# A Mamba-2 recurrence on one core: another PSUM bank for the state's product, and a split diagonal for the group norm's roots

## The chip, the core and the metric

The kernel runs on one core of a Trainium2 chip. The metric is the device time of one execution in microseconds, here the median of three runs. A profiled execution of the same program gives the trace.

The names of the engines in the profile: PE is TensorE (matmuls), PEld is its weight load, DVE is VectorE, ACT is ScalarE, POOL is GpSimd and SP is SyncE, which here only issues DMA transfers. SBUF is the core's working memory. PSUM is the memory into which TensorE writes, eight banks of 128 partitions by 512 float32.

## The reference

A trunk of two layers over 1040 tokens (16 learned tokens and 1024 given ones) of width 1024, in float32. Each layer has a mixer and a convolutional feed-forward part, each between two RMS norms. Layer 0 mixes with a gated linear recurrence beside sliding-window attention. Layer 1, which the change concerns, is a Mamba-2 mixer:

```
z, x, B, C, dt = split(u @ w_in)              # z, x: 2048 wide; B, C: 8 groups x 128; dt: 32 heads
x, B, C = silu(causal_conv4(x, B, C))
for each of 8 groups, with 4 heads of 64 and a state of 128 x 64 a head:
    h[t] = exp(dt[t] * A) * h[t-1] + dt[t] * outer(B[t], x[t])
    y[t] = C[t] . h[t] + D * x[t]
y = y * silu(z)
y = y * rsqrt(mean over the group's 256 channels of y^2 + 1e-6) * w
out = y @ w_out
```

The recurrence is computed in blocks of tokens: inside a block by products of matrices, from block to block through the state.

## The kernel before

**Products.** A float32 GEMM product is made as three matmuls of a reduced float32 type (fp32r in the profile): weights and activations are split into a high and a low half, and high by high, high by low and low by high are summed (`mm3`, lines L251 to L253). Matmuls with plain float32 operands show as two records each.

**Phases.** Layer 0's mixer and feed-forward part, an early share of layer 1's input GEMM, the recurrence with the rest of that GEMM (some 1690 to 2289 us of the span), the output GEMM (tiles `op`) and layer 1's feed-forward part. The order of instructions on each engine is set when the kernel is built: a scheduler places them by priority and by its own estimate of times, and each engine then works through its queue in that order.

**The recurrence.** The loop goes over eight groups:

```python
for g in range(8):
    ssd(g)
    if g > 0:
        z_and_gate(g - 1)
    if g < 7:
        new_tiles(g + 1, range(4))
        make(g + 1, range(4))
z_and_gate(7)
```

`make(g, js)` computes the group's tiles B, C, x0 and x1 (channels by 1040 tokens; `z0` and `z1` for j of 4 and 5) by GEMM, in three chunks of 348 and 346 tokens. The GEMM's PSUM tiles `ps_g` rotate through two banks. `conv4` evacuates them: ACT copies a chunk into a tile `xs_s` (L580, two buffers), ACT takes the first tap (L587) and DVE the other three (L589). Each of x0 and x1 has two buffers, one for even and one for odd groups, so x0 of group g + 2 is written where x0 of group g stood, once that one has been written out. The first taps of x of group g + 2 therefore wait for group g's write to memory.

`ssd(g)` goes over nine blocks of 16 and 8 x 128 tokens. A block's tiles in PSUM have a bank each: `seg` (decays, L1174 and L1181), `tr` (C times B and the transposes of x and B, L1186 and L1188), `py` (outputs: C times the state, L1202, and the block's own part, L1214), and `pst`, which holds the state's product in its upper half (L1204) and the transposes of y in its lower half (L1223). DVE and ACT work between: `wt`, `xdt`, `xw`, the state `st` (POOL's decay L1210, DVE's sum L1211, L1208 in a first block), `y` (L1218, L1219), and L1225 adds y to x.

`gate(g)` multiplies x by z (L1231, DVE, 1026 columns) and then, in three chunks of 342 tokens, squares on ACT (`gsq`, L1236), adds on POOL (L1238) and calls `token_rsqrt`: TensorE sums over channels (`pst_gn`, L178), DVE adds the epsilon (`rs_gn`, L186), POOL takes the power -1/2 (`rr_gn`, L188), and TensorE spreads the root over the partitions by three products with the identity (`rb_gn`, L192). DVE multiplies x by it (L1241). Then x goes to the tensor `zd` in memory (L1244, DMA), from where the output GEMM reads it as `zr`, split by ACT into `zh` (L630) and by DVE into `zl` (L631). `pst_gn` and `rb_gn` take turns in the two banks of the pool `k.pb`; the GEMM's `ps` have two banks and `seg`, `tr`, `py` and `pst` one each, eight in all.

Of the kernel before, what the change touches and what calls it, by code (L numbers as in the profile page):

```python
# [13 lines left out]
F32 = mybir.dt.float32  # L14
F32R = mybir.dt.float32r
AF = mybir.ActivationFunctionType
ALU = mybir.AluOpType
# [4 lines left out]
P = 128  # L22
# [111 lines left out]
def token_blocks(n):  # L134
    nb = (n + 127) // 128
    w = (n + nb - 1) // nb
    return nb, w, [min(j * w, n - w) for j in range(nb)]
# [36 lines left out]
def token_rsqrt(k, acc, col, n, name):  # L174
    nb, w, st = token_blocks(n)
    pst = k.pb.tile([P, 512], F32, tag="pb", name=f"pst_{name}")
    for j in range(nb):
        k.nc.tensor.matmul(pst[:w, j:j + 1], lhsT=acc[:, st[j]:st[j] + w], rhs=col, start=True, stop=True)  # L178
    return rsqrt_rows(k, pst, n, name)


def rsqrt_rows(k, pst, n, name):
    nc = k.nc
    nb, w, st = token_blocks(n)
    s = k.small.tile([P, 4], F32, tag="rs", bufs=3, name=f"rs_{name}")
    nc.vector.tensor_scalar(s[:w, :nb], pst[:w, :nb], 1e-6, None, ALU.add)  # L186
    r = k.small.tile([P, 4], F32, tag="rr", bufs=3, name=f"rr_{name}")
    nc.gpsimd.tensor_tensor(r[:w, :nb], s[:w, :nb], k.mhalf[:w, :nb], ALU.pow)  # L188
    rb = k.pb.tile([P, 512], F32, tag="pb", name=f"rb_{name}")
    for j in range(nb):  # L190
        o = j * w - st[j]
        nc.tensor.matmul(rb[:, j * w:st[j] + w], lhsT=r[:w, j:j + 1].broadcast_to([w, P]),  # L192
                         rhs=k.ident[:w, o:w], start=True, stop=True)
    return rb


# [831 lines left out]
def mixer1(k, W, V, zd, pd):  # L1028
    nc, tc = k.nc, k.tc
    I = k.I  # L1030
    with ExitStack() as es:
# [42 lines left out]
        def dt_chunk(ci, wdt):  # L1074

            t0, n = TCH[ci]
            ps = pp.tile([P, 512], F32, tag="ps", name=f"dtp{ci}")
            for kk in range(NK):
                w = wdt[:, kk * 64:(kk + 1) * 64]
                for i, u in enumerate((k.uh, k.ul)):  # L1080
                    nc.tensor.matmul(ps[:64, :n], lhsT=w, rhs=u[:, kk, t0:t0 + n], start=kk + i == 0, stop=kk + i == NK)
            nc.scalar.copy(dtr[:, t0:t0 + n], ps[:64, :n])
# [82 lines left out]
        def ssd(g):  # L1165
# [4 lines left out]
            for b, (t0, w) in enumerate(BLK):  # L1170
# [30 lines left out]
                if b > 0:  # L1201
                    nc.tensor.matmul(py[:w, 256:512], lhsT=C[:, tk], rhs=st.rearrange("p a b -> p (a b)"), start=True, stop=True)  # L1202
                if b < 8:
                    nc.tensor.matmul(pst[:, 256:512], lhsT=bt[:w], rhs=xw[:w].rearrange("p a b -> p (a b)"), start=True, stop=True)  # L1204
                    ps4 = pst[:, 256:512].rearrange("p (h d) -> p h d", h=4)
                    st2 = t([P, 4, 64], "st", 2, f"st{g}_{b}")
                    if b == 0:
                        nc.scalar.copy(st2, ps4)  # L1208
                    else:
                        nc.gpsimd.tensor_tensor(st2, st, bc(dec, P, b, 64), ALU.mult)  # L1210
                        nc.vector.tensor_tensor(st2, st2, ps4, ALU.add)  # L1211
                    st = st2
# [15 lines left out]
        def gate(g):  # L1228
# [3 lines left out]
            for ci, (t0, n) in enumerate(C1):  # L1232
# [3 lines left out]
                    nc.scalar.activation(s[:, :n], xx[:, t0:t0 + n], AF.Square)  # L1236
                    sq.append(s)
                nc.gpsimd.tensor_tensor(sq[0][:, :n], sq[0][:, :n], sq[1][:, :n], ALU.add)  # L1238
                rb = token_rsqrt(k, sq[0], k.mean_g, n, f"gn{g}_{ci}")
                for j, xx in enumerate((x0, x1)):  # L1240
                    nc.vector.scalar_tensor_tensor(xx[:, t0:t0 + n], xx[:, t0:t0 + n], V["gn"][:, 2 * g + j:2 * g + j + 1],  # L1241
                                                   rb[:, :n], ALU.mult, ALU.mult)
# [117 lines left out]
def build(tc, I, O):  # L1360
# [17 lines left out]
    with ExitStack() as es:  # L1378
# [7 lines left out]
        k.ident = const.tile([P, P], F32, name="ident")  # L1386
        k.mhalf = const.tile([P, 4], F32, name="mhalf"); nc.vector.memset(k.mhalf, -0.5)
        k.tiny = const.tile([P, 1], F32, name="tiny"); nc.vector.memset(k.tiny, 1e-34)
        k.mean_d = const.tile([P, 1], F32, name="mean_d"); nc.vector.memset(k.mean_d, 1 / 1024)
        k.mean_g = const.tile([P, 1], F32, name="mean_g"); nc.vector.memset(k.mean_g, 1 / 256)  # L1390
        off, nv = vec_layout()
# [66 lines left out]
```

## Time and profile before

| | us |
|---|---|
| runs | 3224.03, 3220.53, 3223.37; median 3223.37 |
| profiled execution | 3219.36 |
| its span (first to last instruction) | 3217.5 |
| TensorE's matmuls busy | 3151.6 |
| TensorE's weight loads busy | 3040.0 |
| DVE busy | 2125.0 |
| ACT busy | 1663.5 |
| POOL busy | 456.9 |

The mean granted clock of TensorE over the span is 0.992. Matmuls are pipelined, so that TensorE's busy time in the profile overlaps itself, and a time from one matmul to the next is read from the starts in the timeline. Line numbers in the rows are those of the kernel before; `ps_g<-uh,whi` reads: tile `ps_g` is written from `uh` and `whi`.

### The profile page before, as it was taken

The page shows a single profiled execution, that of the slowest core. Times are in us where ns is not written, and L with a number is a line of the kernel's source. Part 1 is how long each engine was busy: PE and PEld are TensorE (multiplying, and loading weights), DVE is VectorE, ACT ScalarE, POOL GpSimd, SP SyncE. Part 2 cuts the span into 40 slices and gives each one's busy share as a digit, 9 for nine tenths or more (in the row PEclk, how much of TensorE's full clock was granted, in tenths as well). Part 3 has the DMA queues.
Part 4 walks back from the last instruction along what each step waited for, and adds up shares of the span by engine and source line. Part 5 has one row for each costly group of instructions (what it writes and reads, how often), then busy time and mean ns, then how long its engine had stood idle before and what let it go on. Part 6 is the DMA issues. An engine that isn't in the chain of part 4 may idle for free.

```text
span 3217.5 us, 57030 instructions
## 1 busy us (share of the span) xinstructions
PE 3151.6 (98%) x21886; PEld 3040.0 (94%) x21886; DVE 2125.0 (66%) x3998; ACT 1663.5 (52%) x3119; POOL 456.9 (14%) x772
## 2 busy tenths in 40 slices
PE   8999999999999999999999999999999999999998
PEld 7888877999999999999999998999899999999998
DVE  6663334566988885654677767776655798887553
ACT  6764445554544445543446655556455544445442
POOL 3110000332200000320001122221232300000000
PEclk9999999999999999999999999999899999999999
DMA  4221102674322236765432112111466522225673
GB/s 131 80 68 52 35 30 81 190 238 159 111 86 80 77 112 218 231 205 162 140 118 67 40 64 81 63 53 61 145 209 213 159 80 80 80 80 173 199 221 123
DMA packets 186513, 385.71 MB, mean 120 GB/s; under 512 B 22368, under 2 KB 114688, under 8 KB 186240
## 3 DMA queue, kind: packets, MB, share of 16 engines
q1 hardware_dynamic: 186240, 382.06, 37.2%
q8 instruction: 172, 2.82, 0.4%
q14 instruction: 101, 0.83, 0.1%
HBM read 300.89 MB, written 80.50 MB: 119 GB/s over the span
## 4 chain that ended last, share of the span: by engine, by line
PE 85%; issue 4%; ACT 4%; DMA 3%; DVE 3%; POOL 1%; POOLq 0%; SPq 0%; DVEq 0%; ACTq 0%
PE dn L251 4%; PE dn L252 4%; PE dn L253 4%; PE ps_g L252 4%; PE ps_g L251 4%; PE ps_g L253 4%; PE op L253 2%; PE op L252 2%; PE op L251 2%; DMA zr<-zd 2%; PE upS1up L251 2%; PE upS3up L251 2%; PE upA11up L251 2%; PE upA11up L253 2%; PE upS1up L252 2%
## 5 line engine op out<-in xcount | busy, mean ns | idle before, releaser
L108 DVE TENSOR_TENSOR wlo<-wst,whi 128x1024 fp32r<-128x1024 f32 x304 | 379.5, 1251 | 320.9 <-ACT whi L107 293.2
L107 ACT CAST whi<-wst 128x1024 fp32r<-128x1024 f32 x305 | 318.3, 1045 | 376.7 <-PE dn L252 190.0
L251 PE MATMUL dn<-mid,whi 128*128 128x346 f32 (+3 forms) x1056 | 339.0, 321 | 0.0
L253 PE MATMUL dn<-mid,wlo 128*128 128x346 f32 (+3 forms) x1056 | 338.4, 320 | 0.0
L252 PE MATMUL dn<-mid,whi 128*128 128x346 f32 (+3 forms) x1056 | 338.3, 320 | 0.0
L251 PE MATMUL ps_g<-uh,whi 128*128 128x346 f32 (+1 forms) x864 | 288.9, 334 | 1.1 <-ACT xs_s L580 1.1
L252 PE MATMUL ps_g<-ul,whi 128*128 128x346 f32 (+1 forms) x864 | 285.8, 331 | 0.0
L253 PE MATMUL ps_g<-uh,wlo 128*128 128x346 f32 (+1 forms) x864 | 284.2, 329 | 0.2 <-DVE wlo L108 0.2
L253 PE MATMUL op<-zh,wlo 128*128 128x342 f32 (+2 forms) x768 | 249.0, 325 | 2.3 <-DVE wlo L108 2.3
L252 PE MATMUL op<-zl,whi 128*128 128x342 f32 (+2 forms) x768 | 249.0, 325 | 0.9 <-DVE zl L631 0.9
L251 PE MATMUL op<-zh,whi 128*128 128x342 f32 (+2 forms) x768 | 244.3, 325 | 4.1 <-ACT zh L630 3.3
L82 ACT CAST wb<-wst 128x512 fp32r<-128x512 f32 x270 | 165.8, 619 | 131.3 <-PE upS3up L253 57.3
L83 DVE TENSOR_TENSOR wb<-wst,wb 128x512 fp32r<-128x512 f32 x270 | 185.4, 688 | 42.4 <-ACT wb L82 42.3
L252 PEld LDWEIGHTS dn<-mid,whi 128*128 128x128 f32 x1056 | 199.3, 189 | 0.0
L251 PEld LDWEIGHTS dn<-mid,whi 128*128 128x128 f32 x1056 | 199.2, 189 | 0.0
L253 PEld LDWEIGHTS dn<-mid,wlo 128*128 128x128 f32 x1056 | 199.2, 189 | 0.0
L251 PE MATMUL upA11up<-uh,wb 128*128 128x260 f32 (+2 forms) x608 | 171.8, 283 | 0.0
L253 PE MATMUL upA11up<-uh,wb 128*128 128x260 f32 (+2 forms) x608 | 171.4, 282 | 0.0
L252 PE MATMUL upA11up<-ul,wb 128*128 128x260 f32 (+2 forms) x608 | 171.3, 282 | 0.0
L251 PEld LDWEIGHTS ps_g<-uh,whi 128*128 128x128 f32 x864 | 164.5, 190 | 6.4 <-ACT xs_s L580 1.2
L252 PEld LDWEIGHTS ps_g<-ul,whi 128*128 128x128 f32 x864 | 164.1, 190 | 5.2 <-issue 0.9
L253 PEld LDWEIGHTS ps_g<-uh,wlo 128*128 128x128 f32 x864 | 163.8, 190 | 5.4 <-DVE wlo L108 0.7
(537 smaller groups left out, 9485.1 us busy)
## 6 DMA issues: line engine op xcount, KB each, us to landing
wst<-in_dn SPq DMA_DIRECT2D x132, 512.0 KB, 3.8
wst<-in_wo SPq DMA_DIRECT2D x96, 512.0 KB, 3.7
wst<-in_up SPq DMA_DIRECT2D x88, 512.0 KB, 3.6
wst<-in_w SPq DMA_DIRECT2D x74, 512.0 KB, 3.6
md<-cv_u SPq DMA_DIRECT2D x38, 260.0 KB, 2.0
zd<-x SPq DMA_DIRECT2D x16, 513.0 KB, 3.4
zr<-zd SPq DMA_DIRECT2D x48, 171.0 KB, 3.4
mr<-md SPq DMA_DIRECT2D x44, 173.0 KB, 3.9
```

Source lines behind the costliest of these rows:

```text
L82: nc.scalar.copy(p[:, 0], src)
L83: tt(p[:, 1], src, p[:, 0].bitcast(F32), ALU.subtract)
L107: nc.scalar.copy(h, s)
L108: nc.vector.tensor_tensor(l, s, h.bitcast(F32), ALU.subtract)
L251: nc.tensor.matmul(ps, lhsT=wh, rhs=xh, start=start, stop=False, skip_group_check=more)
L252: nc.tensor.matmul(ps, lhsT=wh, rhs=xl, start=False, stop=False, skip_group_check=more)
L253: nc.tensor.matmul(ps, lhsT=wl, rhs=xh, start=False, stop=stop, skip_group_check=more)
```

## The change

For the group norm, `token_rsqrt` gives way to a new function `rsqrt_spread`. Its sums, addition and power are the same. Then POOL multiplies the identity by the root into a tile of 114 rows by 342 columns with three diagonals (`dg`), ACT casts its high half (`dgh`), DVE subtracts to get the low half (`dgl`), and TensorE multiplies a column of ones by each half: two fp32r matmuls of 342 columns in place of three float32 ones of 114.

In `ssd`, the state's product no longer shares a bank with the transposes of y: it has a tile of its own, `pss`, in the pool `k.pb`, beside the gate's `pst_gn` and `rb_gn`. The tile `pst` holds the transposes alone. In the part ahead of the recurrence, the three tiles of the dt projection use the banks of `tr`, `seg` and `py`, where they used the GEMM's.

```diff
--- before.py
+++ after.py
@@ -191,6 +191,31 @@
         o = j * w - st[j]
         nc.tensor.matmul(rb[:, j * w:st[j] + w], lhsT=r[:w, j:j + 1].broadcast_to([w, P]),
                          rhs=k.ident[:w, o:w], start=True, stop=True)
+    return rb
+
+
+def rsqrt_spread(k, acc, col, n, name):
+
+    nc = k.nc
+    nb, w, st = token_blocks(n)
+    assert nb * w == n
+    pst = k.pb.tile([P, 512], F32, tag="pb", name=f"pst_{name}")
+    for j in range(nb):
+        nc.tensor.matmul(pst[:w, j:j + 1], lhsT=acc[:, st[j]:st[j] + w], rhs=col, start=True, stop=True)
+    s = k.small.tile([P, 4], F32, tag="rs", bufs=3, name=f"rs_{name}")
+    nc.vector.tensor_scalar(s[:w, :nb], pst[:w, :nb], 1e-6, None, ALU.add)
+    r = k.small.tile([P, 4], F32, tag="rr", bufs=3, name=f"rr_{name}")
+    nc.gpsimd.tensor_tensor(r[:w, :nb], s[:w, :nb], k.mhalf[:w, :nb], ALU.pow)
+    d = k.work.tile([P, NMAX], F32, tag="pt", bufs=2, name=f"dg_{name}")
+    v = lambda x: x[:w, :n].rearrange("p (j c) -> p j c", c=w)
+    nc.gpsimd.tensor_tensor(v(d), k.ident[:w, :w].unsqueeze(1).broadcast_to([w, nb, w]),
+                            r[:w, :nb].unsqueeze(2).broadcast_to([w, nb, w]), ALU.mult)
+    h, l = (k.work.tile([P, NMAX], F32R, tag="acc", bufs=2, name=f"dg{x}_{name}") for x in "hl")
+    nc.scalar.copy(h[:w, :n], d[:w, :n])
+    nc.vector.tensor_tensor(l[:w, :n], d[:w, :n], h[:w, :n].bitcast(F32), ALU.subtract)
+    rb = k.pb.tile([P, 512], F32, tag="pb", name=f"rb_{name}")
+    for x in (h, l):
+        nc.tensor.matmul(rb[:, :n], lhsT=k.ones[:w].broadcast_to([w, P]), rhs=x[:w, :n], start=x is h, stop=x is l)
     return rb
 
 
@@ -1074,7 +1099,7 @@
         def dt_chunk(ci, wdt):
 
             t0, n = TCH[ci]
-            ps = pp.tile([P, 512], F32, tag="ps", name=f"dtp{ci}")
+            ps = pp.tile([P, 512], F32, tag="ABC"[ci], bufs=1, name=f"dtp{ci}")
             for kk in range(NK):
                 w = wdt[:, kk * 64:(kk + 1) * 64]
                 for i, u in enumerate((k.uh, k.ul)):
@@ -1201,8 +1226,9 @@
                 if b > 0:
                     nc.tensor.matmul(py[:w, 256:512], lhsT=C[:, tk], rhs=st.rearrange("p a b -> p (a b)"), start=True, stop=True)
                 if b < 8:
-                    nc.tensor.matmul(pst[:, 256:512], lhsT=bt[:w], rhs=xw[:w].rearrange("p a b -> p (a b)"), start=True, stop=True)
-                    ps4 = pst[:, 256:512].rearrange("p (h d) -> p h d", h=4)
+                    ps4 = k.pb.tile([P, 512], F32, tag="pb", name=f"pss{g}_{b}")[:, :256]
+                    nc.tensor.matmul(ps4, lhsT=bt[:w], rhs=xw[:w].rearrange("p a b -> p (a b)"), start=True, stop=True)
+                    ps4 = ps4.rearrange("p (h d) -> p h d", h=4)
                     st2 = t([P, 4, 64], "st", 2, f"st{g}_{b}")
                     if b == 0:
                         nc.scalar.copy(st2, ps4)
@@ -1236,7 +1262,7 @@
                     nc.scalar.activation(s[:, :n], xx[:, t0:t0 + n], AF.Square)
                     sq.append(s)
                 nc.gpsimd.tensor_tensor(sq[0][:, :n], sq[0][:, :n], sq[1][:, :n], ALU.add)
-                rb = token_rsqrt(k, sq[0], k.mean_g, n, f"gn{g}_{ci}")
+                rb = rsqrt_spread(k, sq[0], k.mean_g, n, f"gn{g}_{ci}")
                 for j, xx in enumerate((x0, x1)):
                     nc.vector.scalar_tensor_tensor(xx[:, t0:t0 + n], xx[:, t0:t0 + n], V["gn"][:, 2 * g + j:2 * g + j + 1],
                                                    rb[:, :n], ALU.mult, ALU.mult)
@@ -1386,6 +1412,8 @@
         k.ident = const.tile([P, P], F32, name="ident")
         k.mhalf = const.tile([P, 4], F32, name="mhalf"); nc.vector.memset(k.mhalf, -0.5)
         k.tiny = const.tile([P, 1], F32, name="tiny"); nc.vector.memset(k.tiny, 1e-34)
+        one = const.tile([P, 1], F32, name="one"); nc.vector.memset(one, 1.0)
+        k.ones = const.tile([P, 1], F32R, name="ones"); nc.scalar.copy(k.ones, one)
         k.mean_d = const.tile([P, 1], F32, name="mean_d"); nc.vector.memset(k.mean_d, 1 / 1024)
         k.mean_g = const.tile([P, 1], F32, name="mean_g"); nc.vector.memset(k.mean_g, 1 / 256)
         off, nv = vec_layout()
```

The lines move: L186 becomes L206, L188 L208, L204 makes the sums `pst_gn`, L211, L214 and L215 the diagonal and its halves, L218 `rb_gn`; the state's product is L1230, the gate's lines go from L1231, L1236, L1238, L1241 and L1244 to L1257, L1262, L1264, L1267 and L1270; `conv4` from L580, L587 and L589 to L605, L612 and L614.

The scheduler's order changes with it. Names below carry the group's number: `seg4_7` is block 7 of group 4, `gn3_2` the third chunk of the gate of group 3, `ps_g6_0_1` the second chunk of B's GEMM for group 6.

On TensorE, at the third root of gate 3, before:

```order
L1204 MATMUL pst4_4_21965<-xw4_4_21960,bt4_4_21962 128x256
L192 MATMUL rb_gn3_2_22183<-ident_72,rr_gn3_2_22181 128x114 x3
L1174 MATMUL seg4_7_22058<-negm_18239,identr_18240 128x512
L1181 MATMUL seg4_7_22058<-bd_18228,selc_18236 128x512
L1223 MATMUL pst4_4_21965<-ident_72,y4_4_21975 128x128 x2
L1202 MATMUL py4_5_22002<-st4_4_21968,C_4_21464 128x256
L1214 MATMUL py4_5_22002<-xdt4_5_21996,wt4_5_21985 128x64 x4
L1186 MATMUL tr4_7_22066<-C_4_21464,B_4_21463 128x128
```

The root's product stands between blocks of group 4; blocks 5 to 8 are still to come. Now, at the same gate:

```order
L1249 MATMUL pst4_8_22202<-ident_72,y4_8_22208 128x128 x2
L1199 MATMUL seg5_2_22702<-negm_18243,identr_18244 128x512
L1206 MATMUL seg5_2_22702<-bd_18232,selc_18240 128x512
L218 MATMUL rb_gn3_0_22240<-dgh_gn3_0_22236,ones_79 128x342
L204 MATMUL pst_gn3_1_22250<-mean_g_83,gsq3_1_0_22245 114x1 x3
L218 MATMUL rb_gn3_0_22240<-dgl_gn3_0_22237,ones_79 128x342
L218 MATMUL rb_gn3_1_22264<-dgh_gn3_1_22260,ones_79 128x342
L204 MATMUL pst_gn3_2_22274<-mean_g_83,gsq3_2_0_22269 114x1 x3
L218 MATMUL rb_gn3_1_22264<-dgl_gn3_1_22261,ones_79 128x342
L218 MATMUL rb_gn3_2_22288<-dgh_gn3_2_22284,ones_79 128x342
L218 MATMUL rb_gn3_2_22288<-dgl_gn3_2_22285,ones_79 128x342
L276 MATMUL ps_g6_0_1_23090<-uh_87,whi357_22407 128x346
```

All three roots of gate 3 now stand behind the last block of group 4 (`pst4_8`), with two products of group 5 ahead of them and the next GEMM behind them. The first sum, `pst_gn3_0`, stands seven rows above this piece, behind `pss4_7`. In all eight groups the gate's first sum has moved behind the last state product in this way.

On DVE, around the third root of gate 3, before:

```order
L186 TENSOR_SCALAR rs_gn3_2_22179<-pst_gn3_2_22175 114x3
L1225 SCALAR_TENSOR_TENSOR x0_4_21465<-x0_4_21465,vec_81,pst4_3_21927 128x128
L1225 SCALAR_TENSOR_TENSOR x1_4_21466<-x1_4_21466,vec_81,pst4_3_21927 128x128
L1218 TENSOR_TENSOR y4_4_21975<-py4_4_21964,ecs_18233 128x256
L1219 TENSOR_TENSOR y4_4_21975<-y4_4_21975,py4_4_21964 128x256
L1211 TENSOR_TENSOR st4_4_21968<-st4_4_21968,pst4_4_21965 128x256
L1189 TENSOR_TENSOR wt4_6_22023<-wt4_6_22023,tr4_6_22028 128x512
L1193 TENSOR_TENSOR xdt4_6_22034<-tr4_6_22028,dtt_18230 128x256
L1196 TENSOR_TENSOR xw4_6_22036<-tr4_6_22028,dtw_18232 128x256
L1241 SCALAR_TENSOR_TENSOR x0_3_20737<-x0_3_20737,vec_81,rb_gn3_2_22183 128x342
L1241 SCALAR_TENSOR_TENSOR x1_3_20738<-x1_3_20738,vec_81,rb_gn3_2_22183 128x342
```

Between the root's addition and the multiplication by it stands the work of blocks 3 to 6. Now, from the first root on:

```order
L215 TENSOR_TENSOR dgl_gn3_0_22237<-dg_gn3_0_22234,dgh_gn3_0_22236 114x342
L1257 TENSOR_TENSOR x0_4_21546<-x0_4_21546,z0_4_22966 128x1026
L1257 TENSOR_TENSOR x1_4_21547<-x1_4_21547,z1_4_22967 128x1026
L206 TENSOR_SCALAR rs_gn3_1_22254<-pst_gn3_1_22250 114x3
L1267 SCALAR_TENSOR_TENSOR x0_3_20795<-x0_3_20795,vec_85,rb_gn3_0_22240 128x342
L1267 SCALAR_TENSOR_TENSOR x1_3_20796<-x1_3_20796,vec_85,rb_gn3_0_22240 128x342
L215 TENSOR_TENSOR dgl_gn3_1_22261<-dg_gn3_1_22258,dgh_gn3_1_22260 114x342
L206 TENSOR_SCALAR rs_gn3_2_22278<-pst_gn3_2_22274 114x3
...
L1267 SCALAR_TENSOR_TENSOR x1_3_20796<-x1_3_20796,vec_85,rb_gn3_2_22288 128x342
L614 SCALAR_TENSOR_TENSOR x0_5_22297<-xs_s5_2_0_22546,vec_85,x0_5_22297 128x348
L614 SCALAR_TENSOR_TENSOR x0_5_22297<-xs_s5_2_1_22580,vec_85,x0_5_22297 128x346
```

The gate's own steps now follow each other; the two products of gate 4 (L1257) stand between the first root's subtraction and the second's addition, and the taps of x0 of group 5 (L614) behind the last. POOL's queue is of the same kind: between the power and the diagonal of the third root stands the first sum of gate 4 (`gsq4_0`, L1264).

On ACT, at the taps of x0 of group 5, which overwrites x0 of group 3, before:

```order
L587 ACTIVATE x0_5_22193<-xs_s5_2_0_22442,vec_81 128x348
L587 ACTIVATE x0_5_22193<-xs_s5_2_1_22476,vec_81 128x346
L1198 COPY bt4_7_22076<-tr4_7_22066 128x128
L1184 ACTIVATE wt4_8_22099<-seg4_8_22096,ncs_18231 128x128 x4
L580 COPY xs_s5_2_2_22510<-ps_g5_2_2_22485 128x346
L587 ACTIVATE x0_5_22193<-xs_s5_2_2_22510,vec_81 128x346
L580 COPY xs_s6_0_0_22954<-ps_g6_0_0_22929 128x348
```

Blocks 7 and 8 of group 4 still have their copy and exponentials between the taps and the evacuation of the third chunk. Now:

```order
L214 CAST dgh_gn3_2_22284<-dg_gn3_2_22282 114x342
L612 ACTIVATE x0_5_22297<-xs_s5_2_0_22546,vec_85 128x348
L612 ACTIVATE x0_5_22297<-xs_s5_2_1_22580,vec_85 128x346
L605 COPY xs_s5_2_2_22614<-ps_g5_2_2_22589 128x346
L605 COPY xs_s6_0_0_23081<-ps_g6_0_0_23056 128x348
L612 ACTIVATE x0_5_22297<-xs_s5_2_2_22614,vec_85 128x346
L612 ACTIVATE B_6_23046<-xs_s6_0_0_23081,vec_85 128x348
```

The taps stand right behind the last root's cast, with the evacuations of `ps_g5_2_2` and `ps_g6_0_0` behind them; the blocks of group 4 are all ahead of this piece. At the end, the roots of gates 6 and 7 follow each other behind group 7, and on TensorE the output GEMM's first product now stands behind the first root of gate 7, where it stood right behind group 7's last block.

## Rows read from the trace of the kernel before

**Rows 1.** The page's busy times: engine, busy us, share of the span, instructions.

```profile
PE 3151.6 (98%) x21886; PEld 3040.0 (94%) x21886; DVE 2125.0 (66%) x3998; ACT 1663.5 (52%) x3119; POOL 456.9 (14%) x772
```

**Rows 2.** Windows: stretch, length, busy us by engine, PEclk, DMA share, GB/s.

```profile
1850.00:2250.00 400.00, 389.19 (x2591) 367.22 (x2590) 279.81 (x624) 226.39 (x480) 85.08 (x172) 0.99 0.20 65
2255.00:2260.00 5.00, 5.00 (x22) 4.63 (x22) 2.58 (x7) 2.29 (x8) 2.32 (x3) 0.50 0.00 0
2260.00:2265.00 5.00, 5.00 (x33) 4.46 (x33) 3.74 (x10) 1.52 (x5) 1.50 (x2) 0.84 0.00 0
2289.00:2292.00 3.00, 3.00 (x11) 3.00 (x12) 3.00 (x6) 0.96 (x2) 1.38 (x1) 0.50 0.36 90
2293.00:2296.00 3.00, 3.00 (x23) 3.00 (x22) 1.29 (x4) 2.16 (x6) 0.79 (x1) 1.00 0.70 219
```

**Rows 3.** Groups by line, 1740:2310: xcount | busy us, mean ns | idle.

```profile
L1210 POOL TENSOR_TENSOR st<-st,dec 128x256 f32<-128x256 f32 x56 | 37.7, 673 | 136.8 <-DVE st L1211 116.3 <-ACT st L1208 20.0
...
L1238 POOL TENSOR_TENSOR gsq<-gsq,gsq 128x342 f32<-128x342 f32 x24 | 27.0, 1125 | 37.4 <-ACT gsq L1236 37.4
...
L188 POOL TENSOR_TENSOR rr_gn<-rs_gn,mhalf 114x3 f32<-114x3 f32 x24 | 21.4, 890 | 42.9 <-DVE rs_gn L186 42.7
...
L1231 DVE TENSOR_TENSOR x<-x,z 128x1026 f32<-128x1026 f32 x16 | 19.0, 1222 | 0.0
...
L631 DVE TENSOR_TENSOR zl<-zr,zh 128x342 fp32r<-128x342 f32 x14 | 6.2, 510 | 1.7 <-ACT zh L630 1.7
L630 ACT CAST zh<-zr 128x342 fp32r<-128x342 f32 x14 | 5.7, 474 | 6.1 <-PE py L1214 5.4 <-DMA zr<-zd 0.7
...
L186 DVE TENSOR_SCALAR rs_gn<-pst_gn 114x3 f32<-114x3 f32 x24 | 3.7, 155 | 2.5 <-PE pst_gn L178 2.4
```

**Rows 4.** PE timeline, a root's sums and product: start us, us, instruction.

```profile
1988.45 0.67 PE L178 MATMUL pst_gn<-mean_g,gsq 128*114 128x1 f32 x6
1988.98 0.41 PE L251 MATMUL ps_g<-uh,whi 128*128 128x348 f32 x1
...
1994.56 0.82 PE L192 MATMUL rb_gn<-ident,rr_gn 114*128 114x114 f32 x6
1995.22 0.38 PE L1223 MATMUL pst<-ident,y 128*128 128x128 f32 x2
```

**Rows 5.** PE timeline, GEMM products behind a state product.

```profile
1836.52 0.42 PE L251 MATMUL ps_g<-uh,whi 128*128 128x348 f32 x1
1836.78 0.32 PE L252 MATMUL ps_g<-ul,whi 128*128 128x348 f32 x1
1836.94 0.32 PE L253 MATMUL ps_g<-uh,wlo 128*128 128x348 f32 x1
```

**Rows 6.** Chain of waits, gate to GEMM: start us, us, what.

```profile
2078.63 0.49 DVE x L1241
...
2079.14 2.69 DMA zd<-x
...
2081.91 0.69 ACT x L587
...
2086.13 0.46 ACT xs_s L580
...
2086.63 0.43 PE ps_g L251
```

**Rows 7.** Waits of PE, 1740 to 2310 us: total us, times, longest.

```profile
PE tr L1186 <- DVE xdt L1193: 3.8, 2, 1.9
PE pst L1223 <- DVE y L1219: 3.0, 4, 1.1
```

**Rows 8.** PE timeline: a wait, and the end of the recurrence.

```profile
2251.71 0.39 PE L1223 MATMUL pst<-ident,y 16*128 16x16 f32 x2 [2.62 <-ACT st L1208]
2281.67 0.66 PE L1204 MATMUL pst<-xw,bt 128*128 128x256 f32 x2
...
2289.39 0.49 PE L253 MATMUL op<-zh,wlo 128*128 128x342 f32 x1
```

## The prediction

> **What bounds the kernel now.** I read the page's busy times first: TensorE's matmuls fill 98% of the span and its weight loads 94% [rows 1]. The windows say whether that holds where the change acts: in the 400 us of the recurrence TensorE is busy for 389.19 us at a granted clock of 0.99, which is 2.4 GHz, while POOL has 85 us of work and DVE 280 [rows 2]. So here a microsecond counts only if TensorE runs it or waits for it. Its longest waits in the phase are few, 3.8 us and 3.0 us in six places [rows 7]. The phase stays full because three kinds of work stand mixed in its queue: GEMM products of the next group, blocks of this group, the gate of the last. The groups by line then price the gate's steps [rows 3], and the chain of waits shows what stands between a gate and GEMMs two groups later [rows 6].
>
> **What the change removes.** A root's products on TensorE take 0.66 us now, from 1994.56 to 1995.22 [rows 4]. The two that replace them are 342 columns wide, as a GEMM product nearly is, which steps by 0.16 us (1836.78 to 1836.94) [rows 5]. There are 24 roots: 24 x (0.66 - 0.32) = -8.2 us. The order has 181 changes between GEMM and recurrence before and 135 after; a first product behind such a change took 0.26 us in place of 0.16 [rows 5], so 46 x 0.10 = -4.6 us. The waits of rows 7 stood in blocks without GEMM; with GEMM beside those blocks they go, -7 us (bounds 0 and -14, the 6.8 us shown twice over for the shorter waits not shown). Less of the end stands at 1.2 GHz: -3 us, the 2.5 + 0.8 us that the clocks of 0.50 and 0.84 cost in two windows of 5 us [rows 2] (bounds 0 and -3.3). Together -22.8 us.
>
> **What it adds on other engines.** Each root gets a diagonal on POOL, a cast on ACT and a subtraction on DVE. The trace has no such diagonal; its price lies between 0.67 us (a broadcast product of 256 columns, L1210) and 1.13 us (a sum of 342 columns, L1238). I take 1.0, nearer to the row of the same width. The cast is 0.47 (L630) and the subtraction 0.51 (L631) [rows 3]. Beside GEMMs that is hidden, since these engines have idle time. Whether it is hidden is decided by where it stands.
>
> **What it moves.** The state's products now take turns in the two banks that the gate's sums and roots use. In the new order the first sum of gate g-1 stands behind the last state product of group g, in all eight groups; before it stood in the group's first half. For gates 0 to 4 all three roots come as one bunch at a group's end, with no GEMM product between the first root and the third. Behind it comes a GEMM product whose bank is freed by an evacuation that ACT has queued behind the convolution of group g+1, and that convolution overwrites the tile that this gate writes out. TensorE waits three times in such a bunch.
>
> (i) From the first root's high half to the second's: DVE does a subtraction 0.51, then two gate products of the next group 2 x 1.22, then the addition 0.15; POOL a power 0.89 and a diagonal 1.0; ACT a cast 0.47 [rows 3]. That is 5.5, and 5.8 with five handoffs of 0.02 to 0.08 us, as between the pieces of rows 6. TensorE has 0.7 us of work meanwhile, a root's sums (0.53, from 1988.45 to 1988.98 [rows 4]) and the low half, so it idles 5.1 (4.8 to 5.2 by the diagonal's bounds).
>
> (ii) From the second to the third, behind the third's sums: addition 0.15, power 0.89, a sum of the next gate that POOL does ahead of the diagonal 1.13, diagonal 1.0, cast 0.47, handoffs 0.3, less the low half's 0.16: 3.8 (3.5 to 3.9).
>
> (iii) From the third root to the next GEMM: the same chain exists now, from L1241 at 2078.63 to the product at 2086.63, 8.0 us, with the write to memory 2.69, the convolution's first step 0.69 and the evacuation 0.46 [rows 6]. Before, blocks 5 to 8 of the group stood on TensorE beside it; in the new order they stand ahead of it. I take 8.0; without what DVE put between these pieces it would be 5.2.
>
> (iv) TensorE's clock falls after such idling: it idled 2.6 us up to 2251.71 [rows 8], and from 2255 to 2260 the granted clock was 0.50, 1.2 GHz. From 2289 to 2292, at 0.50, it did 11 products where 3 us at 1.00 held 23 [rows 2]: 3 x 12/23 = 1.6 us lost. The two windows of 2255 to 2265 lost 3.3. I take 2.0, nearer to the row whose products are GEMMs.
>
> A bunch is thus 5.1 + 3.8 + 8.0 + 2.0 = 18.9 us (15.1 to 20.4), five of them +94.5 (76 to 102). The sixth, gate 5, has the two last z tiles' GEMMs beside half its chain: +10 (0 to 20). At the end gates 6 and 7 bunch behind group 7. Before, from that group's last state product at 2281.67 to steady products of the output GEMM at 2289.39 it was 7.7 us [rows 8]. That remains, block 8 and the output GEMM's own start. Between the two, TensorE now also waits out two more roots of gate 6 and the first of gate 7, one behind the other: one as in (i) and two as in (ii), 12.7, and 2.0 of clock. From the 14.7 goes the gate's work that leaves group 7's stretch, 3 x (0.66 + 0.53) = 3.6, and 1 us comes for its first blocks, which lose their GEMMs: +12.1 (8 to 17).
>
> **Sum.** 94.5 + 10 + 12.1 - 22.8 = +93.8 us. The profiled execution took 3219.4 us (span 3217.5), 4 us under the median of the three runs; so 3223.4 + 93.8 = 3317 us. With all low bounds it is 76 + 0 + 8 - 30 = +54, with all high ones and the least savings 102 + 20 + 17 - 13 = +126.
>
> **The rivals.** *Milder.* The roots overlap: DVE does the next gate's products and POOL its sum before the first root is due, so that (i) and (ii) cost 1 us together, and only the chain through memory and the clock stay: 5 x (1 + 8.0 + 2.0) = 55, + 5 + 8 - 22.8 = +45, 3268 us (3250 to 3288). For it: DVE and ACT have idle time [rows 2]. Against it: engines take their queues in order, and in the new order those products stand between the first subtraction and the second addition.
>
> *Heavier.* The clock stays at 1.2 GHz through the thin stretches and into the GEMMs, some 10 us a group more: 5 x 8 = +40 on the sum, 3357 us. For it: the clock of 0.50 to 0.84 over 10 us after a single wait [rows 2, 8].
>
> *Faster.* TensorE's work decides and the bunches cost little: work that now runs ahead on other engines has the roots ready when TensorE comes to them, and evacuations run ahead of the memory chain. Then what is left is -22.8: some 3200 us. The point from which it decides is the idle time of a bunch: with six bunches and the end sharing 22.8 us, under 3.3 us each is faster. For it: TensorE's 98% and 94% [rows 1]. Against it: the 2.69 us write alone with its convolution's step is 3.4 us [rows 6], and it can't begin before the third root.
> The Trainium skill, "Perfetto Trace Analysis", section Identifying the Most-Contended Engine, judges TensorE by the share of time that its weight loads are busy, and says to optimise the most contended engine first. By that rule the shorter root products would be the gain, as in this rival, at the 3200 us worked out above. The 94% agrees that TensorE is that engine now; its rows can't say whether it stays fed.
>
> *No change.* The bunches cost just what is saved, 3.3 us each.
>
> The Trainium skill, "TensorE: Matmul & The Clock Gate", section What's actually happening, says that TensorE is throttled by default and that activity releases it. The fall to 0.50 after the wait agrees. By it (iv) belongs to every bunch, as in the sum.
>
> **How the numbers follow.** My forecast has a chance of 0.68, with its own range 3285 to 3345; milder 0.14; heavier 0.08; faster 0.07; no change 0.03. A measurement of this kernel can tell about 0.2%, 6.4 us, from no change. Milder and heavier are slower too, so slower has 0.90, same 0.03, faster 0.07. The range must leave out no more than 2 in 10: from 3258, inside the milder case, to 3356 it leaves out faster and same (0.10), a quarter of the milder and half of the heavier (0.08).
>
> **What would show it.** In the changed profile TensorE's idle time in the recurrence should rise from about 11 to some 100 us, in six places at the groups' ends, with its longest waits at the root products (for the cast, L214 to L218) and at one GEMM product a group (for the evacuation, L605, with the write to memory in its chain). The window of such a group's end should show a clock between 0.5 and 1. The diagonal's row on POOL should have a mean near 1.0 us, the root products a step of 0.16. I am wrong if the waits at the roots are short, if the GEMM behind a bunch starts within 3 us of the third root, or if the phase's end stands where it stood.

## The result, and the profile after

The changed kernel takes 3323.02 us in the median of four runs (3321.5 to 3326.2), the kernel before 3221.95 on the same chip. The ratio is 1.0315, with a 95% interval from 1.0297 to 1.0332: 3.15% slower, +101 us. The forecast was 3317 us. The profiled execution of the changed kernel took 3326.2 us, with a span of 3324.4 and a mean granted clock of 0.972; it is the slowest of the four. Two of the eleven runs of one later version (E10) took 4260 and 6145 us, and its time is the median of the other nine.

The page's busy times of the changed kernel, which answer to [rows 1]:

```profile
PE 3171.7 (95%) x21790; PEld 3054.0 (92%) x21790; DVE 2141.2 (64%) x4023; ACT 1671.7 (50%) x3140; POOL 473.8 (14%) x796
```

TensorE's matmuls were busy for about as long as before, over a longer span, so most of the time came as idling. Nearly all of it lies in the recurrence. From the first `seg` product to steady products of the output GEMM it is 550.9 us before (1738.5 to 2289.4) and 654.9 us after (1740.4 to 2395.3); the phases ahead of it and behind it differ by 2 us at most. In that stretch the gaps between TensorE's matmuls add up to 16.7 us before and 104.7 us after. That is 88 of the 104 us; the other 16 are time in which TensorE was busy, 550.2 us where it had been 534.2.

Waits of TensorE in the changed kernel from 1740 to 2420 us (total us, times, longest), which answer to [rows 7]:

```profile
PE rb_gn L218 <- ACT dgh_gn L214: 48.8, 14, 4.9
PE ps_g L276 <- ACT xs_s L605: 36.5, 5, 7.3
PE tr L1213 <- ACT x L1188: 7.9, 1, 7.9
...
PE ps_g L276 <- ACT z L1172: 3.0, 2, 2.8
```

These are the named places: the roots' casts, the evacuation that ACT has queued behind a convolution, and the first transposes of group 7, which need x of that group. One of the five bunches in TensorE's timeline, between groups 4 and 5:

```profile
2138.68 0.32 PE L218 MATMUL rb_gn<-dgh_gn,ones 114*128 114x342 f32 x1
2138.84 0.67 PE L204 MATMUL pst_gn<-mean_g,gsq 128*114 128x1 f32 x6
2139.42 0.42 PE L218 MATMUL rb_gn<-dgl_gn,ones 114*128 114x342 f32 x1
2144.76 0.66 PE L218 MATMUL rb_gn<-dgh_gn,ones 114*128 114x342 f32 x1 [4.92 <-ACT dgh_gn L214]
2145.21 1.18 PE L204 MATMUL pst_gn<-mean_g,gsq 128*114 128x1 f32 x6
2146.24 0.64 PE L218 MATMUL rb_gn<-dgl_gn,ones 114*128 114x342 f32 x1
2149.66 0.65 PE L218 MATMUL rb_gn<-dgh_gn,ones 114*128 114x342 f32 x1 [2.78 <-ACT dgh_gn L214]
2150.21 0.65 PE L218 MATMUL rb_gn<-dgl_gn,ones 114*128 114x342 f32 x1
2158.17 0.66 PE L276 MATMUL ps_g<-uh,whi 128*128 128x346 f32 x1 [7.31 <-ACT xs_s L605]
2158.62 0.49 PE L277 MATMUL ps_g<-ul,whi 128*128 128x346 f32 x1
...
2160.64 0.49 PE L278 MATMUL ps_g<-uh,wlo 128*128 128x346 f32 x1
2160.93 0.36 PE L276 MATMUL ps_g<-uh,whi 128*128 128x346 f32 x1
```

The three waits of the forecast stand one below the other: 4.92 us for the second root's high half, 2.78 for the third's, 7.31 for the GEMM. The clock is to be seen as well. A product of 346 columns steps by 0.29 us from 2158.62 on and by 0.16 only from 2160.9; a root's sums, 0.58 us at 2138.84, take 1.03 at 2145.21. The windows say the same (stretch, length, busy us by engine, granted clock, DMA share, GB/s):

```profile
2143.00:2148.00 5.00, 2.12 (x8) 1.75 (x8) 2.10 (x5) 0.96 (x2) 2.46 (x4) 0.50 0.45 137
2158.00:2163.00 5.00, 4.83 (x22) 4.83 (x23) 3.19 (x7) 4.05 (x6) 0.91 (x5) 0.70 0.05 19
2163.00:2168.00 5.00, 5.00 (x35) 4.89 (x34) 2.53 (x6) 1.64 (x4) 0.47 (x3) 1.00 0.00 0
```

The granted clock is 0.50, 1.2 GHz, in the bunch, and returns to 1.00 some microseconds after the GEMM has started again. The chain of waits over the last wait, which answers to [rows 6]:

```profile
2147.51 0.87 POOL gsq L1264
2148.38 0.72 POOL dg_gn L211
...
2149.13 0.49 ACT dgh_gn L214
...
2150.90 0.58 DVE x L1267
...
2151.50 2.67 DMA zd<-x
...
2154.25 0.69 ACT x L612
...
2154.96 2.63 DVE x L614 x5
...
2157.67 0.46 ACT xs_s L605
...
2158.17 0.66 PE ps_g L276
```

It is the chain of before, now with nothing on TensorE beside it: the gate's last product, the write to memory (2.67 us), the first tap, five taps on DVE, the evacuation. The prices of the new steps on the other engines, which the forecast had bounded, are in the groups by line (count | busy us, mean ns | idle before):

```profile
L1264 POOL TENSOR_TENSOR gsq<-gsq,gsq 128x342 f32<-128x342 f32 x24 | 24.4, 1015 | 61.4 <-ACT gsq L1262 61.4
...
L211 POOL TENSOR_TENSOR dg_gn<-ident,rr_gn 114x342 f32<-114x342 f32 x24 | 19.4, 806 | 1.2
...
L214 ACT CAST dgh_gn<-dg_gn 114x342 fp32r<-114x342 f32 x24 | 11.4, 477 | 19.3 <-POOL dg_gn L211 19.2
```

And the end of the recurrence on TensorE, answering to [rows 8]:

```profile
2380.94 0.66 PE L218 MATMUL rb_gn<-dgh_gn,ones 114*128 114x342 f32 x1 [4.85 <-ACT dgh_gn L214]
2381.39 1.18 PE L204 MATMUL pst_gn<-mean_g,gsq 128*114 128x1 f32 x6
...
2385.85 0.65 PE L218 MATMUL rb_gn<-dgh_gn,ones 114*128 114x342 f32 x1 [2.78 <-ACT dgh_gn L214]
...
2390.76 0.65 PE L218 MATMUL rb_gn<-dgh_gn,ones 114*128 114x342 f32 x1 [2.79 <-ACT dgh_gn L214]
...
2394.84 0.65 PE L277 MATMUL op<-zl,whi 128*128 128x342 f32 x1 [0.57 <-DVE zl L656]
```

Three more roots, each waited for, stand between group 7's last block and the output GEMM. From the last state product (2369.5) to steady products (2395.3) it is 25.8 us, where it was 7.7.

### The profile page after: what moved, and what is told of

Same layout as the page of the kernel before. It is cut to its first block, busy times and chain, and to the rows that moved or that the text cites. A ratio compares the mean times of both kernels' runs of the same rounds, so it can differ in the third digit from the quotient of the medians.

```text
span 3324.4 us, 56814 instructions
## 1 busy us (share of the span) xinstructions
PE 3171.7 (95%) x21790; PEld 3054.0 (92%) x21790; DVE 2141.2 (64%) x4023; ACT 1671.7 (50%) x3140; POOL 473.8 (14%) x796
## 4 chain that ended last, share of the span: by engine, by line
PE 83%; issue 5%; ACT 4%; DVE 4%; DMA 3%; POOL 2%; SPq 0%; POOLq 0%; DVEq 0%; ACTq 0%
PE dn L276 4%; PE dn L278 4%; PE dn L277 4%; PE ps_g L276 4%; PE ps_g L277 4%; PE ps_g L278 4%; PE op L278 2%; PE op L277 2%; PE op L276 2%; PE upS1up L276 2%; PE upS3up L276 2%; PE upA11up L276 2%; PE upA11up L278 2%; PE upS1up L277 2%; PE upS1up L278 2%
## 5 line engine op out<-in xcount | busy, mean ns | idle before, releaser
L276 PE MATMUL ps_g<-uh,whi 128*128 128x346 f32 (+1 forms) x864 | 290.5, 336 | 39.6 <-ACT xs_s L605 36.5
```

Source lines behind the costliest of these rows:

```text
L276: nc.tensor.matmul(ps, lhsT=wh, rhs=xh, start=start, stop=False, skip_group_check=more)
```

## The experiments

Theory A was that of the prediction, made precise: the two banks of `k.pb` hand out their turns in the order in which the program asks for them. `gate(g - 1)` is written behind `ssd(g)`, so its first sum can't have a bank before the state products of group g have had theirs. This alone makes the bunches, and the waits follow from them. The main rival, B, was the longer root. C and the others belong to single runs. The kernel before was run beside each set: 3220.2 us in the first set, 3221.4 in the second, 3219.9 in the third. The new banks of the dt projection are in all of E1 to E11; E1 (1.0006) and E11 (1.0009) show that they cost nothing that can be measured.

**E1, the new roots alone.** The state's product goes back to the bank of y's transposes:

```diff
-    ps4 = k.pb.tile([P, 512], F32, tag="pb", name=f"pss{g}_{b}")[:, :256]
+    ps4 = pst[:, 256:512]
```

> The new roots and the new banks of the dt projection, with the state's product back in the bank of y's transposes. Theory A (the two shared banks hand their turns out in program order, and that alone puts the gate behind the group's last state product): the roots stand in the groups' first halves again, TensorE's waits for a root's cast (L214) are under 3 us in all, and only the shorter products are left of the change, 24 x 0.34 = 8 us: some 3214 us (3208 to 3222) where before has 3222. Rival B (the longer root, with a diagonal and a cast more, makes the loss wherever it stands): 24 roots x (0.81 + 0.48 + two handoffs) = +32 us, 3254 us.

It took 3222.5 us, ratio 1.0006 (0.9997 to 1.0015): no change, half a microsecond above the range that I gave. Rival B falls: 24 longer roots cost nothing where they are covered, and no wait for a cast is among TensorE's waits. But the 8 us that the shorter products were to save are missing too. The two halves don't stand together in the order, so each is a first product behind other work: by the steps in the trace 42 products take 9.7 us with 0.2 of idling, 0.46 us for a root in place of 0.68. That is -5 us for 24 roots, not -8, and the waits of the blocks came out higher (idle 20.6 us in the recurrence, 16.7 before). The largest are 6.6 us for the decays' exponentials and 6.4 for the state's sum. The profiled execution is the slowest of the eleven, 6 us above their median, so a part of these waits may belong to it alone.

**E2, the new bank alone.** The state's product in `k.pb`, the roots of before:

```diff
-    rb = rsqrt_spread(k, sq[0], k.mean_g, n, f"gn{g}_{ci}")
+    rb = token_rsqrt(k, sq[0], k.mean_g, n, f"gn{g}_{ci}")
```

> The state's product in the norms' pool, with the roots of before (three products with the identity). Theory A: the bunches stay. Each root's chain loses the diagonal and the cast, some 1.4 us, in two waits of each of five bunches and three waits at the end, about 18 us, and gains half of it back as longer products of the roots: 3312 us (3300 to 3322), with 36 us of waits for the evacuation as now. Rival B: near before, 3222 us (3215 to 3235).

It took 3298.2 us, ratio 1.0241 (1.0227 to 1.0255). Its waits:

```profile
PE ps_g L276 <- ACT xs_s L605: 36.9, 5, 7.4
PE rb_gn L192 <- POOL rr_gn L188: 27.8, 18, 3.1
```

So 2.4 of the 3.15% come with the bank alone. The bunches stay, the wait for the evacuation is the same, and the waits for a root fall by 21 us (48.8 to 27.8), in which the diagonal and the cast have gone. I expected 3312 (3300 to 3322), with the gain half given back by longer products at the low clock; the gain was larger, 25 us, and the time fell out of the range. 5.6 of the 25 are the wait for group 7's x (7.9 to 2.3), which I hadn't counted. The products and sums of all 24 roots took 43.3 us in place of 37.0, so 6 of the 21 us were given back.

**E3, the gate between blocks 1 and 2 of the next group.** All of the change; in the program, `z_and_gate(g - 1)` is called inside `ssd(g)`:

```diff
     for b, (t0, w) in enumerate(BLK):
+        if b == 2 and mid is not None:
+            mid()                       # z_and_gate(g - 1)
```

> All of the change, and in the program the gate of group g-1 (with the z products) now stands between blocks 1 and 2 of group g instead of behind block 8; the work is the same. Theory A: the banks' turns then put the roots behind the first two state products, blocks 2 to 8 cover the chain through memory, the waits for the cast and for the evacuation fall below 15 us together, and the time is 3215 us (3205 to 3230). Rival B: the roots are as long as now, 3254 us. Rival C (any state product between two steps of a root in the shared banks makes each wait for the other): the waits move to the middle of the group and the time stays above 3290 us.

It took 3237.1 us, ratio 1.0049 (1.0036 to 1.0061). The same instructions with the same banks, written in another place, took back 86 of the 101 us. Rival C falls, and B with it; the time is 7 us above theory A's range, too. What is left are waits of a smaller kind, for a root behind a root and, in a block, for the copy of B that the state's product reads (L1225 here):

```profile
PE rb_gn L218 <- ACT dgh_gn L214: 10.4, 6, 2.3
PE pss L1232 <- ACT bt L1225: 5.4, 3, 2.2
```

**E4, the state's product in the bank of `seg`.**

```diff
-    ps4 = k.pb.tile([P, 512], F32, tag="pb", name=f"pss{g}_{b}")[:, :256]
+    ps4 = pp.tile([P, 512], F32, tag="B", bufs=1, name=f"pss{g}_{b}")[:, :256]
```

> All of the change, but the state's product takes turns with the decays (seg) in their bank, and not with the gate. Theory A: no bunch, no wait for the evacuation at the groups' ends; a new wait instead, of the next block's seg for DVE's sum of the state, 0 to 0.6 us in 64 blocks: 3214 to 3252 us. Rival B: 3254 us and more, with waits for the cast.

It took 3303.4 us, ratio 1.0259 (1.0245 to 1.0273), far above the 3252 that I gave as the most. The gate's bunches went, as expected: no wait for a cast is among the longest, so this is not rival B either. The waits for the evacuation went down to 7.9 us in five places, not to none. A new wait took their place:

```profile
PE py L1240 <- DVE xdt L1218: 43.7, 26, 3.3
```

The next block's decays can't start before DVE has read this block's state product. Their exponentials then come late, DVE multiplies by them ahead of `xdt` in its queue, and TensorE waits for `xdt`: in one such chain ACT's exponentials take 1.15 us from 2059.63, DVE's product with them 0.69 and `xdt` 0.35, up to TensorE's next product at 2061.97. I had looked only one step down, at `seg` itself (1.3 us there), and not at what stands behind it. In all TensorE idled for 65.3 us of the recurrence (16.7 before) and was busy for 568.4 (534.2 before), at a mean granted clock of 0.92 (0.98 before).

**E5, the same two banks without shared turns.** One tile of `k.pb` is held by the state's product through the whole recurrence; the gate has the other bank to itself:

```diff
+    pss = k.pb.tile([P, 512], F32, tag="pb", name="pss")     # once, ahead of the loop over groups
...
-    ps4 = k.pb.tile([P, 512], F32, tag="pb", name=f"pss{g}_{b}")[:, :256]
+    ps4 = pss[:, :256]
```

> All of the change, with the same two banks in place of the shared turns: one bank of the norms' pool is held by the state's product through the whole recurrence, the other one is left to the gate's sums and roots. Theory A (the loss is the order of turns in shared banks): nothing of the gate is tied to a state product, the roots spread over the blocks, and the waits for the cast, the evacuation and the first transposes all but go: 3218 us (3210 to 3228) against 3220 of before. Rival C (the gate and the state have too few banks, however they are dealt out): one bank for sums and roots makes a root wait for the product of the last one, and the time stays above 3235 us.

It took 3213.6 us, ratio 0.9975 (0.9966 to 0.9985), faster than before by 0.25%. Its longest waits:

```profile
PE seg L1199 <- ACT wt L1209: 6.2, 7, 2.7
PE pst L1249 <- DVE y L1245: 3.6, 5, 1.2
```

With as many banks, the same work and `z_and_gate` where the change has it in the program, the loss is gone: it was the order of turns. Rival C falls a second time.

**E6, the gate's chunks behind blocks 1, 2 and 3.** Shared turns, as in the change, with the gate as a generator that stops ahead of each chunk:

```diff
     for b, (t0, w) in enumerate(BLK):
+        if 1 <= b < 5:
+            next(mid, None)             # z product, then one chunk of the gate of group g - 1
```

> All of the change, shared turns as in it, with the gate's three chunks in the program one behind block 1, 2 and 3 each of the next group. Theory A: a turn ties a root only to a state product near to it, and other blocks stand between the roots, so that the 10 us of waits for the cast that the gate behind block 1 in one piece still had fall below 5: 3224 us (3214 to 3234), below the 3237 of that kernel. Rival C: no better than 3237 us.

It took 3209.5 us, ratio 0.9961 (0.9949 to 0.9974), the fastest version, 4.5 us below the range that I gave: the gain of the product's own bank (E9 to E11) wasn't in it. Its longest waits:

```profile
PE tr L1213 <- DVE xdt L1220: 4.2, 2, 2.2
PE seg L1201 <- ACT wt L1211: 4.1, 3, 2.0
```

No wait for a root's cast or an evacuation is left among them. But TensorE's idling in the recurrence is 16.7 us, as before: in this execution, the fastest of the five, the recurrence is 12.6 us shorter (538.3 us for 550.9) because TensorE was busy for less time. The roots' products and sums in it took 20.0 us in place of 25.7. And the granted clock was low for 7.6 us of it in place of 20.9; at half the clock, the 13.3 us are worth up to 6.7, an estimate. Most of the difference in the clock, 10.2 us, lies at the start of group 7, whose block 0 has its transposes of y at 2251.7 before and at 2236.8 here. Granted clock (third number from the right) in a window around both, before:

```profile
2235.00:2275.00 40.00, 36.64 (x222) 32.79 (x221) 24.60 (x60) 21.41 (x49) 8.20 (x11) 0.87 0.15 53
```

and in this kernel:

```profile
2235.00:2275.00 40.00, 32.71 (x216) 28.31 (x215) 29.59 (x76) 22.48 (x57) 11.16 (x15) 1.00 0.17 58
```

The wait of 2.6 us ahead of the low clock [rows 8], in which the transposes of y waited for ACT to have read the state's product in the same bank, has gone here. That its going keeps the clock up isn't shown: here TensorE waits for 2.0 us at 2252.4, and the clock stays at 1.00.

**E7, the gate writes tiles of its own**, and the transfer to memory starts from them, now in three pieces for each tile (arguments cut at `...`):

```diff
-    nc.vector.scalar_tensor_tensor(xx[:, t0:t0 + n], xx[:, t0:t0 + n], ..., rb[:, :n], ALU.mult, ALU.mult)
+    r = k.work.tile([P, NMAX], F32, tag="hc", bufs=7, name=f"go{g}_{ci}_{j}")
+    nc.vector.scalar_tensor_tensor(r[:, :n], xx[:, t0:t0 + n], ..., rb[:, :n], ALU.mult, ALU.mult)
+    nc.sync.dma_start(zd[2 * g + j][:, t0:t0 + n], r[:, :n])
-for j, xx in enumerate((x0, x1)):
-    nc.sync.dma_start(zd[2 * g + j][:, LEAD:], xx[:, LEAD:])
```

> All of the change, but the gate's last product writes into tiles of its own, from which the transfer to memory starts, so that the convolution two groups later overwrites x without waiting for the transfer. Theory A (the wait for the evacuation is the chain gate, transfer, convolution, evacuation): the wait of 7.3 us a bunch loses the transfer's 2.7, five times: 3310 us (3304 to 3316). Rival D (that GEMM waits for DVE's and ACT's queues behind the roots, and the transfer lies beside it): no change, 3323 us (3318 to 3327).

It took 3316.5 us, ratio 1.0293 (1.0279 to 1.0307); the change has 1.0315 (1.0297 to 1.0332). The time lies between the two ranges, half a microsecond from theory A's, and the two intervals overlap, so the waits have to decide. They and the chain of one bunch:

```profile
PE rb_gn L218 <- ACT dgh_gn L214: 53.5, 18, 4.9
PE ps_g L276 <- ACT xs_s L605: 22.8, 5, 4.6
```

```profile
2143.40 0.58 DVE go L1268
...
2144.00 0.69 ACT x L612
...
2144.71 2.63 DVE x L614 x5
...
2147.42 0.46 ACT xs_s L605
...
2147.92 0.66 PE ps_g L276
```

The transfer is out of the chain and the wait fell from 36.5 to 22.8 us, by the 13.7 that I expected; rival D falls. How much of it reached the time is less sure: the medians differ by 6.5 us, the two profiled executions by 13.2, since the change's is the slowest of its four runs and this one the fastest. The traces show where it went. From the first `seg` product to the GEMM behind the fifth bunch it is 501.0 us in the change and 490.4 here, 10.6 less. The rest is the clock: behind the bunches of the change 18, 10, 17, 9 and 17 steps passed until the GEMM's products stepped by 0.16 us again; here 18, 19, 20, 20 and 21. That is 27 more at 0.29 in place of 0.16, 3.5 us, of which the first four bunches have 3.0. Later, group 7's wait for x fell by 5.6 us, and the roots' waits rose by 4.7 (48.8 to 53.5), most of it at the end, where the order is another: all six roots of gates 6 and 7 now stand ahead of the output GEMM.

**E8, without the product by z**: the gate multiplies two of 1026 columns, so the output lacks the rest of it.

```diff
-    nc.vector.tensor_tensor(xx[:, LEAD:], xx[:, LEAD:], z[:, LEAD:], ALU.mult)
+    nc.vector.tensor_tensor(xx[:, LEAD:LEAD + 2], xx[:, LEAD:LEAD + 2], z[:, LEAD:LEAD + 2], ALU.mult)
```

> All of the change, but the gate multiplies by z in two columns of 1026 alone, so the output lacks the rest of that product. Theory A (between the first and the second root TensorE waits for DVE, which has the next gate's two products ahead of the addition): that wait falls from 4.9 to 2.6 us in five bunches and once at the end, -14 us: 3309 us (3302 to 3315), the wait for the evacuation unchanged at 7.3. Rival E (the first wait is the root's own chain, with the products beside it): no change there, 3321 us.

It took 3306.1 us, ratio 1.0261 (1.0247 to 1.0275), 17 us less than the change in the medians and 21 in the profiled executions.

```profile
PE rb_gn L218 <- ACT dgh_gn L214: 37.5, 15, 3.0
PE ps_g L276 <- ACT xs_s L605: 36.6, 5, 7.3
```

The wait for the casts fell by 11.3 us and the longest of them from 4.9 to 3.0 us; the evacuation's wait didn't move. So in the first wait of a bunch some 1.9 of the 4.9 us belong to DVE's two products of the next gate, and the other 3.0 to the root's own chain; rival E falls. Another 5.6 us are again the wait for group 7's x (7.9 to 2.3 us).

**E9 to E11, what makes E6 faster than before.** The place of the chunks as in E6, with the roots of before (E9), with the product back in the bank of y (E10), and with both undone (E11).

> The kernel with the gate's chunks behind blocks 1, 2 and 3, with the state's product in the norms' pool, but the roots of before. If what made that kernel 0.4% faster than before is the product's own bank, it stays: 3212 us (3207 to 3216), the longer products of the roots costing 24 x 0.2 = 5 us at most. If it is the shorter root, it goes back to 3220 (3216 to 3225).

> The same place of the gate's chunks and the new roots, but the state's product back in the bank of y's transposes. If the product's own bank makes the gain, 3220 us (3215 to 3225), as with the new roots alone in the order of before; if the place of the chunks or the shorter root makes it, 3210 us (3206 to 3214).

> The place of the gate's chunks alone (and the dt projection's banks): old roots, the state's product in the bank of y's transposes. If the place itself makes the gain, 3211 us (3207 to 3215); if not, 3221 us (3216 to 3226), which I expect, since the order of before already had the roots behind blocks 1, 2 and 3.

| | roots of before | new roots |
|---|---|---|
| product in y's bank | E11 3223.9, 1.0009 (1.0000 to 1.0018) | E10 3218.5, 0.9992 (0.9982 to 1.0001) |
| product in `k.pb` | E9 3213.5, 0.9980 (0.9971 to 0.9989) | E6 3209.5, 0.9961 (0.9949 to 0.9974) |

E6 is from the second set, the others from the third. The place of the chunks alone gains nothing. The product's own bank gains 9 to 10 us in either column, clear of the noise. In the profiled pairs a part of that is idling, 17.8 to 14.5 us (E11 to E9) and 22.7 to 16.7 (E10 to E6), and the rest is TensorE's busy time, 534.5 to 528.2 and 527.0 to 521.6; with it the granted clock is low for 8 and 10 us less (22.0 to 13.7 and 17.1 to 7.6); why it is, stays open. The new roots gain 4 to 5 us in either row, at the edge of the noise, and nothing in the order of before (E1). So the product's bank is a small gain that the order of turns buried, and the new root at best a smaller one.

## Why the prediction was right, point by point

**The mechanism.** Right, and shown: undoing the turns alone takes the loss away (E5) or all but 16 us of it (E3), undoing the root alone (E2) leaves three quarters. What the prediction read off the order, TensorE waiting in the bunches behind each group, is where the time lies. That the sum came within 7 us of the measured +101 is in part luck: two errors of 12 and 22 us had opposite signs (see the savings).

**The three waits of a bunch.** Forecast 5.1, 3.8 and 8.0 us; measured 4.92, 2.78 and 7.31. The second was too high by two prices on POOL, the sum at 0.87 in place of 1.13 and the diagonal at 0.72 in place of 1.0, and by the low half, which at 1.2 GHz covered 0.49 us of the chain in place of 0.16; the handoffs were shorter, too. The mean of the diagonal is 0.81 us, so the nearer bound was the broadcast product of 0.67, not the sum of the same width. The first came out near by luck: DVE's two products of the next gate took 1.48 us each in the mean where the forecast had 1.22, and the shorter diagonal and TensorE's own work of 1.0 us beside it (0.7 in the forecast) made up for that. Removing those two products takes 1.9 us off the first wait (E8), removing the transfer 2.7 off the third (E7).

**The clock.** Forecast 2.0 us a bunch. The 71 steps at the low clock behind the five bunches are 71 x 0.13 = 9.2 us, 1.85 a bunch. That term left out the work within a bunch, which runs at 1.2 GHz too: a root's sums took 1.03 us for 0.58.

**The sixth bunch.** Forecast 10; the waits for x (7.9) and for z's evacuation (3.0) are 10.9 us. In E2, E7 and E8 the wait for x is 2.3 us; what takes the 5.6 away there stays open.

**The end.** Forecast +12.1, measured 25.8 - 7.7 = +18.1. The waits were over-estimated, if anything (4.85 + 2.78 + 2.79 against 12.7); what was missed is the low clock, 0.50 from 2376.0 to 2399.9, where a root's own products and sums took 2.1 us (from 2380.94 to 2.78 us ahead of 2385.85) and in a bunch at full clock 1.2 (from 2138.68 to 4.92 us ahead of 2144.76).

**The savings.** The step that failed, though the sum held: -22.8 us. Its -7 for the blocks' waits came: without the rows named above, TensorE idled 8.5 us, where it was 16.7. Its other -15.8, on TensorE's own work, did not. Covered, the shorter root products are worth -5, not -8.2 (E1), and in the bunches nearly all of them ran at the low clock: the products and sums of the 24 roots took 37.0 us net of idling, where they had taken 29.4, +7.6. The -3 for less of the end at 1.2 GHz had the wrong sign, and the -4.6 for fewer changes between GEMM and recurrence is shown by no run. TensorE's work as a whole took 16 us more. The idling, 88 us more, was below the 100 that the forecast's waits give (five times 16.9, 10 and 12.7, less 7). The rest of the forecast was -6 where +16 came. So two errors, -12 and +22 us, left one of 10 in the recurrence of the profiled pair and 7 in the medians. The idling before, named as about 11 us, is that of the window of 400 us; in the whole recurrence it is 16.7.

**The rivals.** Milder failed on the first wait: DVE didn't run ahead, its queue stood as written. Heavier failed because the clock came back within 18 steps of the GEMM, 5.3 us. Faster needed less than 3.3 us of idling a bunch; it was 15. With the order undone, E5 and E6 give 8 and 12 us, a third to a half of its 22.8.

## What to carry to other kernels

In this kernel a pool's banks were handed out in program order (E3, E5), so a tile that was added to a shared pool inside a loop of nine blocks put the pool's users that are written behind the loop behind its last turns, wherever the scheduler would have moved them. Look at the order first: if a dependent chain stands without independent matmuls beside it, price it as a sum of latencies, and price the matmuls in it at the low clock, as measured here (a root's sums 1.03 us for 0.58). Where a tile needs a bank of its own, give it one by holding it, or write the other user's requests at the place where they are to run.

## What the runs showed that I had not expected

Within the bunches, a shorter wait did not give back its whole length. In E7 the wait before the GEMM was 4.57 us where it had been 7.31, and the GEMM then ran 18 to 21 steps of 0.29 us instead of 9 to 18. The stretch at 0.50 was as long in both, at the bunch around 2150 in the change (first) and in E7:

```profile
2140.50:2161.00 20.50, 6.15 (x20) 5.16 (x21) 11.00 (x22) 6.93 (x12) 5.63 (x10) 0.50 0.43 139
2133.40:2153.90 20.50, 9.30 (x31) 8.30 (x32) 11.98 (x23) 8.06 (x13) 5.62 (x11) 0.50 0.43 130
```

From the third root to full speed that bunch took 11.3 us in the change (2149.66 to 2160.93) and 11.7 in E7 (2142.16 to 2153.86), though 20 products of the GEMM were done in it in place of 9. By this the five waits, 13.7 us shorter, gave 10.6 by the time that the fifth was over. The medians of the whole kernel, 6.5 us apart, are too near each other for a finer account.
